# A 32-byte tile ahead of one buffer group: the weight buffers of the feed-forward stage start 32 bytes lower in SBUF

## The chip, the cores and the metric

One core of a Trainium2 chip runs the whole program. Times are device microseconds (us) of one execution; a profiled execution also gives a trace with start and duration of every instruction. SBUF is the on-chip working memory, 128 partitions wide. An address below is a byte offset within a partition, as the built program lays the tiles out. Engines: PE = TensorE (matmuls; its weight loads have a row of their own, PEld), DVE = VectorE, ACT = ScalarE, POOL = GpSimd, SP = SyncE, which issues most DMAs.

## The reference

One encoder layer on two sequences of 1024 tokens, width 1024: low-rank attention with 4 heads beside a Fourier mixing branch, one shared output projection, then a SwiGLU feed-forward block. All in float32.

```
x = x + ga1 * (concatenate([y_mla, y_four], axis=-1) @ w_out)
h2 = rmsnorm(x, g_ffn) * (1.0 + sc2) + sh2
ffn = (jax.nn.silu(h2 @ w_gate) * (h2 @ w_up)) @ w_down        # 1024 -> 2816 -> 1024
x = x + ga2 * ffn                                               # then a last rmsnorm
```

## The kernel before

**Products.** float32 values are split into a high part (rounded to the PE's fp32r type) and a low remainder: `split` (L63 on ACT, L64 on DVE). Each product of two split operands is a triple of matmuls, `mm3`: L79 high x high, L80 high x low, L81 low x high. In `mm3(out, lh, ll, rh, rl)` the l operands are the stationary weights, 128 x 128, loaded ahead of each matmul, and the r operands stream through as the moving operand, 128 x 512.

**Stages.** Up to about 300 us: modulation vectors, input projection, Fourier branch. About 300 to 750 us: attention (scores at L1216 to L1220, whose moving operand is `lat`, and whose weights are `qa` and `qp`) and the output projection (moving `wv`, weights `o0b`, `o1b`). Then the feed-forward block, for sequence 0 and then for sequence 1, with a Strassen-like scheme of 7 products in place of 8:

- The gate/up stage has 22 steps n, one for each 128 of the 2816 hidden columns. A step runs 7 products (`step`, `prod`) of 4 triples each. The moving operand is `H[k]`, kept in SBUF for the whole stage; the weights are `wh`, `wl`, made anew for each product by `hl`. So both sequences together have 2 x 22 x 7 x 4 = 1232 triples. POOL and DVE form the combinations of the weights (`rgu`, `val`) for the next step. During sequence 0 POOL also prepares combinations of `w_down` (`down_combos`, buffer `tdb`).
- The down stage has products of 11 chunks (`prod2`) with 4 triples each, where both operands are `wh` and `wl` tiles. The last product of sequence 1 uses operands that were split ahead and kept in the tiles of `H` (`held`).

**Where the tiles lie.** The pool of `w` (L1359, "p5", with the `H` tiles, `X0` and `X1`, the latter two holding `rgu` and later `draw`) sits at the lower end of SBUF from address 11840; each of its tiles has 8192 bytes in a partition, so all of them start at a multiple of 64. The pool of `w5` (L1501, "p5b") is allocated from the upper end, 229344, which is 32 above a multiple of 64. From the top down it holds 18 `val` buffers of 2048 bytes (lowest at 192480), 8 `wl` buffers of 2048, `ga`/`tdb` and `gf` of 4096 each, and 8 `wh` buffers of 2048. `wl` therefore begins at 176096 and `wh` at 151520; all of the pool lies 32 above a multiple of 64. The order in which the tags of `w5` are first asked for is set inside `hl`.

`hl` waits for nothing of its own: `wh` and `wl` have 8 buffers each, a step uses 7, and a product's pair is made while the same product of the step before runs. The instruction order is the program's own, held by `tc.issue_after` and `first` at some places.

Of the kernel before, what the change touches and what calls it, by code (L numbers as in the profile page):

```python
# [12 lines left out]
F32 = mybir.dt.float32  # L13
# [8 lines left out]
P = 128  # L22
# [31 lines left out]
def hybrid_encoder_kernel(ctx: ExitStack, tc: tile.TileContext, a: dict):  # L54
# [4 lines left out]
    def rd(t):  # L59
        return t.bitcast(F32)  # L60

    def split(hi, lo, src, eng=None):
        here["a"] = nc.scalar.copy(hi, src).ins  # L63
        here["v"] = (eng or nc.vector).tensor_tensor(out=lo, in0=src, in1=rd(hi), op=ALU.subtract).ins  # L64
# [751 lines left out]
    S = {}  # L816
# [541 lines left out]
    with ExitStack() as st:  # L1358
# [142 lines left out]
        w5 = st.enter_context(tc.tile_pool(name="p5b", bufs=1, side="right", reuse_waits="tile"))  # L1501
# [8 lines left out]
        def hl(v):  # L1510
            h = w5.tile([P, 512], F32R, tag="wh", name="wh", bufs=8)
            if "gf" not in S:
                S["gf"] = w5.tile([P, D], F32, name="gf")
                w5.tile([P, 2, 512], F32, tag="ga", name="tdb", bufs=1)
            l = w5.tile([P, 512], F32R, tag="wl", name="wl", bufs=8)
            split(h, l, v)
            return h, l

# [3 lines left out]
        for s in range(2):  # L1522
# [71 lines left out]
            if s == 0:  # L1594
                wts = [hl(w0[i]) for i in range(4)]
                with behind():
                    for _ in range(2):
                        next(prep)
            else:
                wts = first_w  # L1600
            A = {}
            late = None
            for n, f in enumerate(order):
# [10 lines left out]
                def step(j, ps, k, first, src=src):  # L1614
                    prod(ps, k, cur[j], first)
                    if s == 0 and n == 0:
                        if j == 0:
                            cur.extend(hl(v) for v in w0[4:])
                            w0.clear()
                            S["n3"] = norm3(1, S.pop("jk3").bitcast(BF16))  # L1620
# [11 lines left out]
                        for i in ((), (), (), (0, 1), (2, 3), (4,), (5, 6))[j]:  # L1632
                            nxt.append(hl(src[i]))
# [351 lines left out]
```

## Time and profile before

| | |
|---|---|
| Median of 3 runs | 2051.51 us (2048.66 to 2051.56) |
| Profiled execution, own time | 2051.31 us |
| Its span, first to last instruction | 2049.5 us |
| Mean granted PE clock | 0.996 |
| Gate/up, sequence 0 and 1 | about 750 to 1155 and 1390 to 1835 us |
| Down, sequence 0 and 1 | about 1155 to 1390 and 1835 to 2049 us |

In the rows of the trace, "L79 PE MATMUL bank<-H,wh" is an instruction of line 79 on PE that writes a tile named bank from H and wh; L81's rows name wl as the weight. A matmul's recorded duration runs past the start of the next one, since matmuls are pipelined; the distance from one start to the next tells what one costs. Three numbers with strokes are the shortest, the median and the longest duration in ns.

### The profile page before, as it was taken

What the parts mean: (1) busy time and instruction counts of PE and PEld (TensorE: products, weight loads), DVE (VectorE), ACT (ScalarE), POOL (GpSimd) and SP (SyncE); (2) the same over time, 40 slices, a digit from 0 to 9 for tenths busy, and PEclk for the clock granted to TensorE, in tenths of its full rate; (3) what the DMA queues carried; (4) which work ended last, traced back from release to release, by engine and by line L of the source; (5) the groups of instructions that cost most, each with busy time, mean ns of one, the idle gap of its engine ahead of it and who ended that gap; (6) DMA issues with size and microseconds to landing.
All of it is one profiled execution on the core that took longest, in us unless ns stands there. A gap on an engine that the chain in (4) does not pass through costs nothing.

```text
span 2049.5 us, 28369 instructions
## 1 busy us (share of the span) xinstructions
PE 2006.0 (98%) x9910; PEld 1641.6 (80%) x9910; DVE 1397.2 (68%) x2076; ACT 890.5 (43%) x1732; POOL 827.0 (40%) x972
## 2 busy tenths in 40 slices
PE   7899999999999999999999999999999999999998
PEld 3778778888888878888888888877888888888876
DVE  4568758666677778767777577688665665667585
ACT  2675436555555563333232365454323333336441
POOL 0564213112313237878878311234544444420142
PEclk9999999999999999999999999999999999999999
DMA  9786884444544475555455587674322322258662
GB/s 387 256 317 211 293 307 116 111 99 113 146 102 143 139 268 202 174 194 186 174 172 186 168 305 249 216 233 162 132 93 88 117 90 103 94 182 277 221 231 95
DMA packets 183036, 376.64 MB, mean 184 GB/s; under 512 B 17996, under 2 KB 57548, under 8 KB 179052
## 3 DMA queue, kind: packets, MB, share of 16 engines
q1 hardware_dynamic: 165548, 321.33, 45.9%
q0 software_dynamic: 17344, 53.49, 8.7%
q8 instruction: 78, 1.28, 0.2%
q14 instruction: 66, 0.54, 0.1%
HBM read 262.75 MB, written 120.39 MB: 187 GB/s over the span
## 4 chain that ended last, share of the span: by engine, by line
PE 55%; DVE 3%; DMA 2%; issue 1%; POOL 1%; ACT 0%; SPq 0%; DVEq 0%; ACTq 0%; POOLq 0%
PE bank L81 18%; PE bank L79 18%; PE bank L80 18%; DVE wl L64 1%; DVE val L137 1%; DMA draw<-s_d 1%; POOL val L137 0%; DMA val<-x_d 0%; DVE val L1782 0%; DMA draw<-t_d 0%; ACT wh L63 0%; DVE val L134 0%; POOL rs_y L105 0%; DVE H L64 0%; DMA rgu<-in_wgu_dram 0%
## 5 line engine op out<-in xcount | busy, mean ns | idle before, releaser
L79 PE MATMUL bank<-H,wh 128*128 128x512 f32 x1232 | 487.5, 396 | 2.4 <-DVE val L137 0.9
L81 PE MATMUL bank<-H,wl 128*128 128x512 f32 x1232 | 488.6, 397 | 0.2 <-DVE wl L64 0.2
L80 PE MATMUL bank<-H,wh 128*128 128x512 f32 x1232 | 484.4, 393 | 0.3 <-DVE H L64 0.3
L79 PEld LDWEIGHTS bank<-H,wh 128*128 128x128 f32 x1232 | 231.2, 188 | 58.6 <-DVE val L137 1.8
L80 PEld LDWEIGHTS bank<-H,wh 128*128 128x128 f32 x1232 | 231.3, 188 | 58.1 <-DVE H L64 0.6
L81 PEld LDWEIGHTS bank<-H,wl 128*128 128x128 f32 x1232 | 231.3, 188 | 56.9 <-DVE wl L64 0.5
L64 DVE TENSOR_TENSOR wl<-draw,wh 128x512 fp32r<-128x512 f32 x286 | 202.7, 743 | 85.6 <-ACT wh L63 85.2
L137 DVE TENSOR_TENSOR val<-bank,val 128x512 f32<-128x512 f32 x200 | 136.7, 689 | 158.8 <-PE bank L81 153.4
L63 ACT CAST wh<-draw 128x512 fp32r<-128x512 f32 x286 | 168.6, 619 | 159.3 <-PE bank L80 82.9
L137 POOL TENSOR_TENSOR val<-val 128x512 f32<-128x512 f32 x58 | 84.0, 1456 | 365.5 <-DVE val L1756 188.8
L80 PE MATMUL bank<-wl,wh 128*128 128x512 f32 x572 | 223.6, 391 | 2.3 <-DVE wl L64 2.3
L63 ACT CAST wh<-rgu 128x512 fp32r<-128x512 f32 x172 | 106.8, 621 | 269.5 <-PE bank L80 209.5
L81 PE MATMUL bank<-wh,wl 128*128 128x512 f32 x572 | 222.6, 389 | 0.0
L79 PE MATMUL bank<-wh 128*128 128x512 f32 x572 | 222.6, 389 | 0.0
L63 ACT CAST wh<-val 128x512 fp32r<-128x512 f32 x133 | 82.2, 621 | 269.8 <-PE bank L80 253.1
L64 DVE TENSOR_TENSOR wl<-val,wh 128x512 fp32r<-128x512 f32 x133 | 130.8, 985 | 77.3 <-ACT wh L63 77.3
L64 DVE TENSOR_TENSOR wl<-rgu,wh 128x512 fp32r<-128x512 f32 x172 | 166.8, 970 | 3.7 <-ACT wh L63 3.7
L134 POOL TENSOR_TENSOR val<-rgu 128x512 f32<-128x512 f32 x80 | 117.7, 1472 | 100.9 <-DMA rgu<-in_wgu_dram 97.2
L80 PEld LDWEIGHTS bank<-wl,wh 128*128 128x128 f32 x572 | 107.3, 188 | 27.4 <-DVE wl L64 5.4
L79 PEld LDWEIGHTS bank<-wh 128*128 128x128 f32 x572 | 107.4, 188 | 22.4
L81 PEld LDWEIGHTS bank<-wh,wl 128*128 128x128 f32 x572 | 107.4, 188 | 22.2
L1225 DVE TENSOR_REDUCE mx<-ps_s 128x1 f32<-128x1024 f32 x64 | 78.2, 1222 | 61.3 <-PE ps_s L1220 60.9
(385 smaller groups left out, 4048.4 us busy)
## 6 DMA issues: line engine op xcount, KB each, us to landing
rgu<-in_wgu_dram SPq DMA_DIRECT2D x86, 512.0 KB, 4.4
draw<-s_d SPq DMA_DIRECT2D x143, 256.0 KB, 3.8
s_d<-val POOLq DMA_DIRECT2D x88, 256.0 KB, 3.9
draw<-t_d SPq DMA_DIRECT2D x88, 256.0 KB, 4.2
s_d<-val SPq DMA_DIRECT2D x66, 256.0 KB, 2.4
draw<-in_w_down_dram SPq DMA_DIRECT2D x55, 256.0 KB, 4.6
wada<-in_w_ada_dram SPq DMA_DIRECT2D x11, 1024.0 KB, 10.5
xt<-in_x_dram SPq DMA_DIRECT2D x16, 512.0 KB, 10.3
```

The costliest lines, as they stand in the source:

```text
L63: here["a"] = nc.scalar.copy(hi, src).ins
L64: here["v"] = (eng or nc.vector).tensor_tensor(out=lo, in0=src, in1=rd(hi), op=ALU.subtract).ins
L79: nc.tensor.matmul(out, lh, rh, start=first, stop=False, skip_group_check=cont)
L80: nc.tensor.matmul(out, lh, rl, start=False, stop=False, skip_group_check=cont)
L81: here["t"] = nc.tensor.matmul(out, ll, rh, start=False, stop=last, skip_group_check=cont).ins
L134: return eng.tensor_tensor(out=out, in0=x, in1=y, op=ALU.subtract).ins
L137: eng.tensor_tensor(out=out, in0=x, in1=y, op=ALU.add)
L1225: nc.vector.tensor_reduce(out=mx, in_=ps, axis=AX.X, op=ALU.max)
```

## The change

```
             l = w5.tile([P, 512], F32R, tag="wl", name="wl", bufs=8)
+            if "edge" not in S:
+                S["edge"] = w5.tile([P, 8], F32, name="edge")
             split(h, l, v)
```

`edge` has 8 float32 values, 32 bytes, in a partition. It is asked for once, after the `wl` buffers, and lies between the lowest `val` buffer and the highest `wl` buffer, at 192448. Nothing reads or writes it. The `val` buffers and the tiles of `w` keep their places. `wl` now begins at 176064, `ga`/`tdb` at 171968, `gf` at 167872, `wh` at 151488: all four groups 32 bytes lower, and at multiples of 64.

No instruction is added, removed or moved on any engine. The pool before it in the same space (output projection: `wv0` from 155616 to 172000, `wv1` up to 188384) is now overlapped 32 bytes off its tile borders, so two first uses wait differently. On SP, at the head of the feed-forward stage, where the first `tdb` and `gf` are loaded, before:

```order
L1528 DMA val<-in_wgu_dram 128x512 [waits DMAHW5_49]
L1528 DMA val<-in_wgu_dram 128x512 [waits DMAHW6_49]
L1528 DMA val<-in_wgu_dram 128x512 [waits DMAHW7_49,PE_49]
L1551 DMA tdb<-in_w_down_dram 128x1024 [waits DMAHW0_49,PE_49]
L1690 DMA gf<-in_g_final_dram 128x1024 [waits DMAHW1_49,PE_49]
```

and after the change (its line numbers are 2 higher):

```order
L1530 DMA val<-in_wgu_dram 128x512 [waits DMAHW5_49]
L1530 DMA val<-in_wgu_dram 128x512 [waits DMAHW6_49]
L1530 DMA val<-in_wgu_dram 128x512 [waits DMAHW7_49,PE_49]
L1553 DMA tdb<-in_w_down_dram 128x1024 [waits DMAHW0_49,PE_49]
L1692 DMA gf<-in_g_final_dram 128x1024 [waits DMAHW1_49]
```

`tdb` now touches `wv0` as well as `wv1` and waits for one matmul more of the output projection (PE's count 4190 in place of 4189); POOL's first operation on `tdb` does too. `gf` needs no wait on PE any more, since `tdb`, ahead of it on SP, has already waited for that matmul.

## The prediction

> **What bounds the kernel now.** I read the page first: busy shares, then the chain that ended last.
>
> ```profile
> span 2049.5 us, 28369 instructions
> PE 2006.0 (98%) x9910; PEld 1641.6 (80%) x9910; DVE 1397.2 (68%) x2076; ACT 890.5 (43%) x1732; POOL 827.0 (40%) x972
> PE 55%; DVE 3%; DMA 2%; issue 1%; POOL 1%; ACT 0%; SPq 0%; DVEq 0%; ACTq 0%; POOLq 0%
> ```
>
> PE is busy for 98% of the span and leads the chain. So the question is what a matmul costs, not who waits. The busy time by stages (PE alone; start and end, busy us, count, granted clock, DMA share, GB/s) says it more sharply: two stretches of gate/up, one of down.
>
> ```profile
> 800.00:1100.00 300.00, 300.00 (x1288) 1.00 0.53 183
> 1440.00:1740.00 300.00, 300.00 (x1288) 1.00 0.29 103
> 1170.00:1290.00 120.00, 120.00 (x529) 1.00 0.77 264
> ```
>
> PE never stops in any of them and the clock is full, but gate/up starts 1288 matmuls in 300 us, some 233 ns each, and down 529 in 120 us, some 227 ns. All are 128 x 128 by 128 x 512. The rows by line give the exact period, from the first and the last start and the count: gate/up of sequence 0, of sequence 1, down, and the last product, where both operands are tiles of `H`.
>
> ```profile
> L79 PE MATMUL bank<-H,wh x429: 392/392/392, 799.9 to 1099.5; 128*128 128x512 f32 x143
> L79 PE MATMUL bank<-H,wh x429: 399/399/399, 1439.9 to 1739.5; 128*128 128x512 f32 x143
> L79 PE MATMUL bank<-wh x148: 389/389/389, 1189.7 to 1289.6; 128*128 128x512 f32 x148
> L79 PE MATMUL bank<-H x20: 389/389/389, 2026.7 to 2039.6; 128*128 128x512 f32 x20
> ```
>
> A triple (L79, L80, L81) takes 299.6/428 = 0.7000 us in gate/up, in both sequences, 99.9/147 = 0.6796 us in down and 12.9/19 = 0.679 us in the last product. Within a row every duration is the same, shortest to longest, although DMA, DVE and POOL load differ widely between the stretches. So the extra 20.4 ns are no contention with another engine that comes and goes; they belong to what PE itself reads.
>
> What differs is the address of the two operands. Take each address modulo 64. Down: weights and moving operand both at 32. Last product: both at 0. Gate/up: weights at 32 (`wh`, `wl`), moving operand at 0 (`H`). Writing into one bank many times is not the reason: the last product does that too. Neither 0 nor 32 is slow by itself; the case in which the two differ is.
>
> The attention scores test this inside one loop. Their weights `qa` and `qp` lie at 0 modulo 64 in both sequences; the moving `lat` lies at 0 for sequence 0 and, in other tiles, at 32 for sequence 1. First and last matmul of an undisturbed run of each:
>
> ```profile
> 302.51 0.39 PE L1219 MATMUL ps_s<-lat,qp 128*128 128x512 f32 x1
> 306.14 0.39 PE L1220 MATMUL ps_s<-lat,qp 128*128 128x512 f32 x1
> 539.70 0.39 PE L1216 MATMUL ps_s<-lat,qa 128*128 128x512 f32 x1
> 541.81 0.40 PE L1220 MATMUL ps_s<-lat,qp 128*128 128x512 f32 x1
> ```
>
> Sequence 0: 16 periods in 3.63 us, 0.2269 us each. Sequence 1: 9 periods in 2.11 us, 0.2344 us. The same lines with weights at the same place cost 7.5 ns more per matmul when the moving operand is 32 bytes off the weights' phase. Gate/up has 0.7000/3 = 0.2333, down 0.6796/3 = 0.2265: the same two levels. That is the ground of the forecast, with one reservation. Over the whole of both sequences the recorded durations of one such line (sequence 0, then 1) lie closer:
>
> ```profile
> L1219 PE MATMUL ps_s<-lat,qp x64: 387/393/397, 302.5 to 503.2; 128*128 128x512 f32 x64
> L1219 PE MATMUL ps_s<-lat,qp x62: 392/394/400, 513.1 to 714.8; 128*128 128x512 f32 x62
> ```
>
> The shortest differ by 5 ns, the medians by 1. There other shapes interrupt the scores every few periods; nothing interrupts gate/up, so the undisturbed runs weigh more.
>
> **The change part by part.**
>
> *Gate/up weights against H.* `wh` and `wl` move from 32 to 0 modulo 64, `H` stays at 0, and the phases agree as they do in down. At down's period a triple saves 0.7000 - 0.6796 = 0.0204 us; 1232 triples save 25.1 us. PE is 100% busy there, so nothing hides it: it comes off the end, unless another engine becomes late. The next in line, over each whole gate/up stage (PE, PEld, DVE, ACT, POOL busy):
>
> ```profile
> 750.00:1155.00 405.00, 403.58 (x1736) 324.20 (x1735) 300.30 (x304) 137.09 (x228) 310.96 (x280) 1.00 0.54 186
> 1390.00:1835.00 445.00, 443.96 (x1904) 356.82 (x1903) 280.97 (x344) 140.79 (x243) 205.11 (x191) 1.00 0.32 111
> ```
>
> Half of the saving, 12.6 us, falls on the first row: 405 becomes 392, of which POOL is busy 311 (79%) and DVE 300 (77%). Each pair of weights is made a whole step ahead, 28 x 0.7 = 19.6 us. I cost new waits at nothing; without this cover POOL would have to grow by 81 us before it set the pace.
>
> *A finer offset.* Take weights minus moving operand modulo 512 bytes, one row of a weight tile. It is 0 in down and in the last product, 416 in gate/up now, 384 after the change. No 512-column run at 384 is in the trace. The Fourier projection has short runs of 256 columns whose moving `wcs` steps by 2144 bytes, so that the offset changes from triple to triple. Here is the start of three such triples, each with the start that follows it:
>
> ```profile
> 133.84 0.28 PE L79 MATMUL bank<-wcs_h,eoh 128*128 128x256 f32 x1
> 134.22 0.28 PE L79 MATMUL bank<-wcs_h,eoh 128*128 128x256 f32 x1
> ...
> 134.93 0.28 PE L79 MATMUL bank<-wcs_h,eoh 128*128 128x256 f32 x1
> 135.28 0.28 PE L79 MATMUL bank<-wcs_h,eoh 128*128 128x256 f32 x1
> ...
> 136.32 0.28 PE L79 MATMUL bank<-wcs_h,eoh 128*128 128x256 f32 x1
> 136.68 0.36 PE L79 MATMUL bank<-wz_h,eoh 128*128 128x448 f32 x1
> ```
>
> The first triple has offsets 160, 416, 160 and takes 0.38 us; the second, 384, 128, 384, takes 0.35; the third, 0, 256, 0, takes 0.36. So 384 is as good as 0 here, and the slow one is that with 416. I take 384 as 0. The bounds are the rivals below: nothing gained, or 10 ns a triple better still.
>
> *Down weights and moving operand.* Both shift by 32, so the offset stays 0. Their common phase goes from 32 to 0, which the last product already has: 0.679 against 0.6796. Cost 0, with bounds of 0.6 ns on 572 triples, 0.3 us either way.
>
> *Splits.* DVE reads its first input at the old place and `wh` at the new one. Rows of the first down stage: `draw` at 0 with `wh` at 32, and `H` tiles at 0 alone.
>
> ```profile
> L64 DVE TENSOR_TENSOR wl<-draw,wh x153: 678/689/1811, 1165.4 to 1389.4; 128x512 fp32r<-128x512 f32 x153
> L64 DVE TENSOR_TENSOR H<-H,H x24: 679/686/1850, 1188.9 to 1231.1; 128x512 fp32r<-128x512 f32 x24
> ```
>
> Medians of 689 and 686 ns: at most 3 ns on some 600 splits, 1.8 us of DVE time that lies beside PE. Cost 0. The same answer holds for ACT's casts, POOL's work on `tdb` and the loads into `tdb`, `gf` and `ga`: same sizes, off PE's path, in stages where POOL and ACT have 94 and 268 of 405 us free.
>
> *Waits at the head.* The first `tdb` load and POOL's first `tdb` operation wait for one more matmul of the output projection. Its last low x high matmul on PE, the load's issue on SP, POOL's operation:
>
> ```profile
> 747.82 0.39 PE L81 MATMUL gb<-wv,o1b 128*128 128x512 f32 x1
> 750.86 0.99 SPq L1551 DMA_DIRECT2D tdb<-in_w_down_dram  x1
> L134 POOL TENSOR_TENSOR tdb<-tdb x1: 2282/2282/2282, 759.5 to 759.5; 128x512 f32<-128x512 f32 x1
> ```
>
> The matmul ends at 748.2, 2.6 us before SP comes to that load, and POOL comes 9 us later still. Queued behind the load on SP are `gf`, which nobody needs before the down stage, and `X0`. Cost 0; without the cover, one matmul, 0.23 us.
>
> Sum: -25.1 us. The profiled execution took 2051.31 us, 1.8 outside its span and 0.2 under the median of the runs, so 2051.3 - 25.1 = **2026.2 us**.
>
> **The rivals.**
>
> 1. *Part of it.* Agreeing phases need not give down's period. The input projection (448 columns) has weights and moving operand both at 0 modulo 64, with offsets 0 and 256. Four of its triples, and six 256-column matmuls to take the cost of a column from:
>
> ```profile
> 138.74 0.36 PE L79 MATMUL bank<-wz_h,eoh 128*128 128x448 f32 x1
> 141.17 0.36 PE L79 MATMUL bank<-wz_h,eoh 128*128 128x448 f32 x1
> 306.37 0.28 PE L79 MATMUL gb<-ql,wq_h 128*128 128x256 f32 x1
> 306.96 0.28 PE L81 MATMUL gb<-ql,wq_l 128*128 128x256 f32 x1
> ```
>
> A triple takes 2.43/4 = 0.6075 us. 256 columns take 0.59/5 = 0.118, so a column costs (0.2269 - 0.118)/256 = 0.43 ns, and 448 columns at the fast level would make a triple of 3 x (0.2269 - 64 x 0.00043) = 0.598. It has 9 ns more. If gate/up settles there, it saves 11 ns on each of 1232 triples, 14 us: **2037 us**. The medians of L1219, 1 ns apart, would put the low end of this at 3 ns a triple, 3.7 us, or 2047.6.
>
> 2. *Nothing.* The 20 ns stem from something that the shift leaves alone, such as the distance of the two pools in SBUF: **2051.3 us**. For it: in down and in the last product both operands lie in one pool, in gate/up in two. Against it: the three `wcs` triples above use the same tiles and take different times. [...]
>
> 3. *Slower.* The offset counts modulo 512 and 384 is worse than 416 at 512 columns. Place: every gate/up triple. Price: as much above today's as today's is above down's, 20.4 ns x 1232 = 25.1 us, **2076 us**. It decides from 3.3 ns a triple on (4.1 us). Against it: 0.35 us at 384 and 0.38 at 416 with 256 columns.
>
> 4. *More.* 384 beats 0, as 0.35 against 0.36 would have it; 5 to 10 ns a triple more, 6 to 12 us: **2014 to 2020 us**.
>
> **How the numbers follow.** Forecast 0.64 (its own range 2023 to 2030), part 0.14, nothing 0.10, more 0.08, slower 0.04. From 2018 to 2042 lie the forecast, most of "part" and some of "more": about 0.8. A measurement of this kernel tells 0.2%, 4.1 us, from no change. Faster by more: 0.64 + 0.08 + 0.13 of "part" = 0.85. Within: 0.10 and 0.01 of "part" = 0.11. Slower: 0.04.
>
> **What would show it.** The first and last start of L79 in a stretch of gate/up: 0.680 us a triple if I am right, 0.700 if nothing happens, 0.689 for part, 0.72 for slower; some 1323 matmuls in 300 us in place of 1288. Gate/up shorter by 12 to 13 us in each sequence; the down stages, and all before 745 us, as long as now. DVE's and ACT's medians in the splits within 5 ns. It would be wrong if the triple changes by another amount, if PE begins to wait for `wl` or `val` inside gate/up, or if the down triple leaves 0.680.

## The result, and the profile after

The changed kernel takes **2050.26 us** (median of 12 runs, 2046.51 to 2054.73) and the kernel before 2051.66 us (median of 12 runs, 2048.66 to 2055.99): ratio 0.9994, 95% interval 0.9984 to 1.0004. That is no change that can be measured. The forecast was 2026.2, with a range from 2018 to 2042, so it was wrong by the whole expected gain. The profiled execution took 2049.49 us itself.

From the page of the changed kernel, the span and the busy shares, and from the view by stretches of time the same three stretches as before (busy time of PE, PEld, DVE, ACT and POOL, then granted clock, DMA share, GB/s):

```profile
span 2047.7 us, 28368 instructions
PE 2002.2 (98%) x9910; PEld 1641.1 (80%) x9910; DVE 1386.5 (68%) x2076; ACT 891.3 (44%) x1732; POOL 831.1 (41%) x972
```

```profile
800.00:1100.00 300.00, 300.00 (x1288) 241.34 (x1287) 211.15 (x216) 90.89 (x152) 237.87 (x215) 1.00 0.53 183
1440.00:1740.00 300.00, 300.00 (x1292) 243.26 (x1292) 173.56 (x215) 91.30 (x154) 149.01 (x125) 1.00 0.29 102
1170.00:1290.00 120.00, 120.00 (x529) 99.09 (x528) 84.86 (x125) 65.95 (x117) 13.25 (x12) 1.00 0.76 259
```

PE is as full as before and the clock is full. Gate/up of sequence 0 starts 1288 matmuls in 300 us, exactly as before; 1323 were expected. Sequence 1 has 1292, four more. The rows of L79 in the changed kernel, for gate/up of sequence 0 and 1, for down, and for the last product (count, then shortest/median/longest duration in ns, then first and last start):

```profile
L79 PE MATMUL bank<-H,wh x429: 392/398/398, 800.2 to 1099.8; 128*128 128x512 f32 x143
L79 PE MATMUL bank<-H,wh x430: 390/393/404, 1440.3 to 1739.4; 128*128 128x512 f32 x144
L79 PE MATMUL bank<-wh x148: 389/389/389, 1189.9 to 1289.8; 128*128 128x512 f32 x148
L79 PE MATMUL bank<-H x27: 389/389/389, 2020.1 to 2037.8; 128*128 128x512 f32 x27
```

A triple takes 299.6/428 = 0.7000 us in sequence 0, 299.1/429 = 0.6972 in sequence 1, 99.9/147 = 0.6796 in down and 17.7/26 = 0.68 in the last product. The average of sequence 0 has not moved by a nanosecond, and yet the shift did reach PE: before, each L79 there had the one duration 392; now the durations alternate between 392 and 398. Something in the rhythm changed, and the mean did not. That the mean of sequence 1 fell by 2.8 ns is worth 616 x 0.0028 = 1.7 us, less than what runs of one kernel differ by.

### The profile page after: what moved, and what is told of

The parts are those of the page before. It is cut to its first block, busy times and chain, and to the rows that moved or that the text cites. A ratio compares the mean times of both kernels' runs of the same rounds, so it can differ in the third digit from the quotient of the medians.

```text
span 2047.7 us, 28368 instructions
## 1 busy us (share of the span) xinstructions
PE 2002.2 (98%) x9910; PEld 1641.1 (80%) x9910; DVE 1386.5 (68%) x2076; ACT 891.3 (44%) x1732; POOL 831.1 (41%) x972
## 4 chain that ended last, share of the span: by engine, by line
PE 55%; DVE 3%; DMA 2%; issue 1%; POOL 1%; ACT 1%; SPq 0%; DVEq 0%; ACTq 0%; POOLq 0%
PE bank L80 18%; PE bank L81 18%; PE bank L79 18%; DVE wl L64 1%; DVE val L137 1%; DMA draw<-s_d 1%; DMA val<-x_d 0%; POOL val L137 0%; DMA draw<-t_d 0%; DVE val L1784 0%; ACT wh L63 0%; DVE val L134 0%; DMA X<-hc_d 0%; POOL rs_y L105 0%; DVE val L1773 0%
## 5 line engine op out<-in xcount | busy, mean ns | idle before, releaser
L79 PE MATMUL bank<-H,wh 128*128 128x512 f32 x1232 | 486.8, 395 | 2.3 <-DVE val L137 1.0
L80 PE MATMUL bank<-H,wh 128*128 128x512 f32 x1232 | 486.5, 395 | 0.3 <-DVE H L64 0.3
L81 PE MATMUL bank<-H,wl 128*128 128x512 f32 x1232 | 486.3, 395 | 0.2 <-DVE wl L64 0.2
L79 PEld LDWEIGHTS bank<-H,wh 128*128 128x128 f32 x1232 | 231.7, 188 | 59.1 <-DVE val L137 1.9
L81 PEld LDWEIGHTS bank<-H,wl 128*128 128x128 f32 x1232 | 231.7, 188 | 55.7 <-DVE wl L64 0.5
L80 PEld LDWEIGHTS bank<-H,wh 128*128 128x128 f32 x1232 | 231.7, 188 | 55.5 <-DVE H L64 0.6
L137 POOL TENSOR_TENSOR val<-val 128x512 f32<-128x512 f32 x58 | 83.6, 1450 | 365.8 <-DVE val L1758 189.1
L80 PE MATMUL bank<-wl,wh 128*128 128x512 f32 x572 | 223.6, 391 | 4.1 <-DVE wl L64 4.1
L81 PE MATMUL bank<-wh,wl 128*128 128x512 f32 x572 | 222.7, 389 | 0.0
L79 PE MATMUL bank<-wh 128*128 128x512 f32 x572 | 222.6, 389 | 0.0
L64 DVE TENSOR_TENSOR wl<-rgu,wh 128x512 fp32r<-128x512 f32 x172 | 155.1, 902 | 3.7 <-ACT wh L63 3.7
L80 PEld LDWEIGHTS bank<-wl,wh 128*128 128x128 f32 x572 | 107.4, 188 | 29.6 <-DVE wl L64 7.3
L79 PEld LDWEIGHTS bank<-wh 128*128 128x128 f32 x572 | 107.4, 188 | 22.4
L81 PEld LDWEIGHTS bank<-wh,wl 128*128 128x128 f32 x572 | 107.4, 188 | 21.9
L134 POOL TENSOR_TENSOR val<-val 128x512 f32<-128x512 f32 x89 | 119.4, 1359 | 1.3
```

Source lines behind the costliest of these rows:

```text
L79: nc.tensor.matmul(out, lh, rh, start=first, stop=False, skip_group_check=cont)
L80: nc.tensor.matmul(out, lh, rl, start=False, stop=False, skip_group_check=cont)
L81: here["t"] = nc.tensor.matmul(out, ll, rh, start=False, stop=last, skip_group_check=cont).ins
L134: return eng.tensor_tensor(out=out, in0=x, in1=y, op=ALU.subtract).ins
L137: eng.tensor_tensor(out=out, in0=x, in1=y, op=ALU.add)
```

## Theories

The shift can have done nothing to the period for three reasons. **Distance:** the two addresses do not matter, the 20 ns come from the two pools as such, and the shift leaves the cause alone. **Modulus:** the offset between weights and moving operand matters, and only 0 is good, counted modulo 512 or 256; 384, which the change reached, is then still a disagreement. **Coarse places:** some offsets are good and some bad, in a way that is not just "0 or not". In what follows the offset is `wh` minus `H`, and "triple" is the period of L79 in a stretch of gate/up, as above. `wh_only` and `h_up` put the tile `edge` elsewhere, and `e160_p3` adds a second tile; all the other kernels change only the size of `edge`.

## The experiments

### e416 and e160: offset 0, and offset 256

`edge` of 416 bytes brings the offset to 0; 160 bytes bring it to 256, which is 0 modulo 256 only.

```
-                S["edge"] = w5.tile([P, 8], F32, name="edge")
+                S["edge"] = w5.tile([P, 104], F32, name="edge")
```

> The untouched tile has 416 bytes in place of 32, so that the weights' offset to the moving H, modulo 512, is 0 (before: 416; after the change: 384). Theory A, the offset modulo 512 decides: the gate/up triple falls to the down stage's 0.680 us and the time to about 2026 us. Theory B, the distance of the two pools or the structure of the gate/up loop decides: triple 0.700 us, about 2050 us, whatever the offset.

```
-                S["edge"] = w5.tile([P, 8], F32, name="edge")
+                S["edge"] = w5.tile([P, 40], F32, name="edge")
```

> Offset 256 modulo 512, a tile of 160 bytes. Theory A in its coarse form (only 0 is good): triple 0.697 to 0.700 us, about 2050 us. If multiples of 256 count as 0: 0.680 us and 2026 us. Theory B: 0.700 us.

e416: 2031.52 us (4 runs, 2029.97 to 2032.15) against 2053.32 of the kernel before on the same chip (7 runs), ratio 0.9895, interval 0.9878 to 0.9911. e160, a single run: 2030.68 us. L79 in gate/up of sequence 1, first e416, then e160:

```profile
L79 PE MATMUL bank<-H,wh x441: 389/389/389, 1440.3 to 1739.5; 128*128 128x512 f32 x147
```

```profile
L79 PE MATMUL bank<-H,wh x442: 389/389/389, 1440.1 to 1740.0; 128*128 128x512 f32 x148
```

299.2/440 = 0.6800 and 299.9/441 = 0.6800 us a triple: down's period, and down's one duration, 389. So the offset does set the period of gate/up, which is against "distance". And 256 is as good as 0 here, 0.6800 against 0.6800, so the modulus is not 512.

What becomes of the gain is read from the same run of e416. 1232 triples x 0.0200 are 24.6 us; the span fell by 2049.5 - 2028.1 = 21.4. The view of waits on PE from 745 us on (us in total, times, longest), three of its rows, of the kernel before and then of e416, where L1664 is the line that was L1662:

```profile
PE bank L80 <- DVE wl L64: 2.3, 3, 0.9
PE bank L79 <- DVE val L137: 0.9, 2, 0.5
...
PE bank L79 <- DVE val L1662: 0.5, 1, 0.5
```

```profile
PE bank L80 <- DVE wl L64: 2.1, 3, 0.9
PE bank L79 <- DVE val L1664: 1.9, 2, 1.7
PE bank L79 <- DVE val L137: 1.6, 2, 0.9
```

PE waits 1.9 + 1.6 - 0.5 - 0.9 = 2.1 us more for `val`, which DVE makes: a tenth of the gain goes into these waits. Of the remaining 1.1 us, 0.6 is a later start of gate/up (748.6 against 748.0 us); the rest is within what executions differ by.

### e288 and e64: two other offsets

```
-                S["edge"] = w5.tile([P, 8], F32, name="edge")
+                S["edge"] = w5.tile([P, 72], F32, name="edge")
```

> Offset 128 modulo 512, a tile of 288 bytes. If the sign of the offset makes no difference it should be as the changed kernel with 384 (0.697 to 0.700 us, about 2050 us). Theory A with multiples of 128 counting as 0 is already excluded by 384. Theory B: 0.700 us.

```
-                S["edge"] = w5.tile([P, 8], F32, name="edge")
+                S["edge"] = w5.tile([P, 16], F32, name="edge")
```

> Offset 352 modulo 512, phase 32 modulo 64 as before the change, a tile of 64 bytes. If the phase modulo 64 has any part in it, the fixed pattern of three as before, 0.700 us. If each offset has a period of its own, another value between 0.680 and 0.720 us. Theory B: 0.700 us.

e288 (offset 128): 2048.52 us, a single run. e64 (offset 352, or 96 modulo 256): 2056.24 us, a single run. Gate/up of sequence 0, e288 and then e64:

```profile
L79 PE MATMUL bank<-H,wh x430: 390/393/404, 800.3 to 1099.4; 128*128 128x512 f32 x144
```

```profile
L79 PE MATMUL bank<-H,wh x427: 392/397/400, 800.2 to 1099.6; 128*128 128x512 f32 x143
```

299.1/429 = 0.6972 and 299.4/426 = 0.7028 us. Offset 128 repeats what the changed kernel (384, the same modulo 256) has in sequence 1, down to the three durations 390/393/404. No phase modulo 64 is left as an explanation: 128 and 384 are both 0 modulo 64 and slow, 0.6972 us in e288 and 0.7000 and 0.6972 in the changed kernel.

### wh_only: two of the three operand pairs agree

The tile stands between `wh` and `gf`, so that only `wh` moves (offset 0), and `wl` keeps 160.

```
             if "gf" not in S:
+                S["edge"] = w5.tile([P, 40], F32, name="edge")
                 S["gf"] = w5.tile([P, D], F32, name="gf")
...
             l = w5.tile([P, 512], F32R, tag="wl", name="wl", bufs=8)
-            if "edge" not in S:
-                S["edge"] = w5.tile([P, 8], F32, name="edge")
             split(h, l, v)
```

> The tile has 160 bytes and lies between the wh buffers and gf, so that only wh moves: its offset to H modulo 256 becomes 0, that of wl stays 160, and wh and wl stand 160 apart. Theory N: a matmul pays when the weights loaded during it (those of the next matmul) are off the moving operand it reads. Then one of three gate/up matmuls pays (L80, before wl), the triple is about 0.687 us, and down keeps 0.680, since every load there still agrees. Theory O: a matmul pays when its own weights are off. Then L81 pays in gate/up (also 0.687), and in down L80 and L81 pay, 0.693. Time by N about 2036 us, by O about 2044 us.

A single run: 2058.89 us, beside 2050.43 of the kernel before. The three lines of gate/up of sequence 1, and then L79 of down:

```profile
L79 PE MATMUL bank<-H,wh x429: 396/397/398, 1440.2 to 1739.8; 128*128 128x512 f32 x143
```

```profile
L80 PE MATMUL bank<-H,wh x429: 393/396/396, 1439.7 to 1739.3; 128*128 128x512 f32 x143
```

```profile
L81 PE MATMUL bank<-H,wl x429: 392/392/396, 1440.0 to 1739.6; 128*128 128x512 f32 x143
```

```profile
L79 PE MATMUL bank<-wh x129: 389/393/397, 1190.3 to 1279.3; 128*128 128x512 f32 x129
```

Gate/up stays at 299.6/428 = 0.7000 us, although two of three matmuls read weights at offset 0. Down, whose `wh` and `wl` no longer agree with each other, goes to 89.0/128 = 0.695. In down two of the three pairs disagree: L80, whose weights are `wh` and whose moving operand is a `wl` tile, and L81, where it is the other way round. Both theories of the expectation fall: neither a price on each matmul with its own weights nor a price on each with the weights loaded for the next gives a full 0.7000 with two of three pairs in agreement. In gate/up one disagreeing pair in the triple costs the whole price of 20 ns; in down two of them cost 15. Beside the trace of the kernel before, whose span is 7.6 us shorter, down takes 3.0 us more in sequence 0 and 3.8 in sequence 1 from its first to its last L79. That is 6.8 us, where 15 ns on each of 572 triples would be 8.6, so not all of the price shows in the time. Gate/up also begins 1.2 us later.

### h_up: the other side moves

The weights stay where the kernel before has them, 32 above a multiple of 64; the tiles of `H` go up by 160 bytes to meet them.

```
+        S["edge"] = w.tile([P, 40], F32, name="edge")
         for tag in ("H20", "X0", "X1", "H21", "H30", "H31", "H00", "H41", "H01", "H50", "H51", "H10", "H11", "H40", "H60", "H61"):
...
-            if "edge" not in S:
-                S["edge"] = w5.tile([P, 8], F32, name="edge")
```

> The other operand is moved instead: a tile of 160 bytes stands at the head of the lower pool, so that H, X0 and X1 lie 160 bytes higher and wh and wl stay where they were before the change. Offset modulo 256 is 0, phase of the weights 32 modulo 64 and of H 32. If only the offset counts: gate/up triple 0.680 us, about 2031 us. If the weights' own address counts: 0.700 us and 2051 us.

A single run: 2036.22 us, beside 2050.43 of the kernel before. Gate/up of sequence 1:

```profile
L79 PE MATMUL bank<-H,wh x442: 389/389/389, 1439.8 to 1739.7; 128*128 128x512 f32 x148
```

299.9/441 = 0.6800 us, the period that e160 has with the weights moved by the same 160 bytes. So in gate/up it is the offset between the two and not the place of either. (The time stands above e416's because this execution came to gate/up later: its first matmul on `H` starts at 753.8 us, in e416 at 748.6. From there to the program's last matmul the two take 1271.2 and 1270.1 us.)

### e256, e192, e352, e384: what repeats, and whether any offset but 0 is good

```
-                S["edge"] = w5.tile([P, 8], F32, name="edge")
+                S["edge"] = w5.tile([P, 64], F32, name="edge")
```

> A tile of 256 bytes, offset 160 modulo 512. If the offset counts modulo 256, this is the kernel before to the last ns: triple 0.700 us with the same pattern of three, about 2051 us. If 512 is the modulus, it is a place of its own, between 0.680 and 0.705.

```
-                S["edge"] = w5.tile([P, 8], F32, name="edge")
+                S["edge"] = w5.tile([P, 48], F32, name="edge")
```

> A tile of 192 bytes, offset 224 modulo 256, 32 short of agreement. If the cost grows with the distance from agreement: between 0.680 and 0.697 us a triple, about 2040 us. If every disagreement costs the same: about 0.700 us, 2051 us.

```
-                S["edge"] = w5.tile([P, 8], F32, name="edge")
+                S["edge"] = w5.tile([P, 88], F32, name="edge")
```

> A tile of 352 bytes, offset 64 modulo 256. If only 0 is good: 0.697 to 0.703 us a triple, about 2050 us. If the curve is symmetric about 0 and grows with distance, below 0.700.

```
-                S["edge"] = w5.tile([P, 8], F32, name="edge")
+                S["edge"] = w5.tile([P, 96], F32, name="edge")
```

> A tile of 384 bytes, offset 32 modulo 256, the smallest disagreement on the other side of 0. Offset 224 gave 0.700 us. If only 0 is good: 0.697 to 0.703 us, about 2050 us.

Single runs: 2058.96 and 2053.32 us (beside 2050.43 of the kernel before), then 2058.65 and 2052.98 us (beside 2054.74). They differ by what lies ahead of the feed-forward stage: gate/up begins at 753.3, 748.7, 754.2 and 748.5 us, and from there to the program's last matmul all four take 1293 to 1294 us, the kernel before 1292. Gate/up of sequence 0 in e256, e192, e352, e384:

```profile
L79 PE MATMUL bank<-H,wh x429: 392/392/392, 799.7 to 1099.3; 128*128 128x512 f32 x143
```

```profile
L79 PE MATMUL bank<-H,wh x429: 393/394/397, 799.7 to 1099.3; 128*128 128x512 f32 x143
```

```profile
L79 PE MATMUL bank<-H,wh x429: 393/398/398, 799.7 to 1099.3; 128*128 128x512 f32 x143
```

```profile
L79 PE MATMUL bank<-H,wh x430: 395/396/396, 799.6 to 1099.9; 128*128 128x512 f32 x144
```

All four have 0.7000 us a triple. e256, a shift of exactly 256 from the kernel before, repeats even its one duration of 392. That confirms the modulus from a slow offset, as e160 did from the good one.

In sequence 1, e352 has the same mean in another form. Apart from one wait, every distance there is 233 or 234 ns, and the durations no longer alternate:

```profile
L79 PE MATMUL bank<-H,wh x428: 394/394/497, 1440.6 to 1739.6; 128*128 128x512 f32 x143
```

An even rhythm is thus no mark of the fast level, 0.680 us a triple; the distance from start to start tells.

The table gathers what the traces show. The last column is the pattern of the distances from one start to the next, in ns, read off consecutive starts of the trace, in sequence 0 where nothing else is said; a pattern repeats to 1 ns:

```
offset mod 256   kernels             triple, us   distances
0                e416, e160, h_up    0.680        226, 227, 227
32               e384                0.700        231 or 232, 235
64               e352 (seq. 0)       0.700        231, 235 or 236
64               e352 (seq. 1)       0.700        233 or 234
96               e64                 0.703        repeats after 7 matmuls
128              after (seq. 0)      0.700        229, 238
128              after (seq. 1)      0.697        repeats after 7 matmuls
128              e288                0.697        repeats after 7 matmuls
160              before, e256        0.700        231, 231, 238
224              e192                0.700        231, 235, 234, 234
0 and 160        wh_only             0.700        repeats after 9 matmuls
```

192 was not tried. The multiples of 32 that were tried fall into two classes: 0 with 0.680 us a triple, and the six others with 0.697 to 0.703.

### e160b and e160_p3: the gain timed, and the same cure tried in attention

e160b is e160 again. e160_p3 adds a 160-byte tile in the pool of the attention stage, so that `lat` of sequence 1 comes from offset 96 to 0 against `qa` and `qp`; the probabilities `pt`, the moving operand of the values, shift with it.

```
                 S["pt", s, b, h] = [w.tile([P, 8, 2, P], F32R, tag=f"pt{k}", name=f"pt{k}", bufs=2) for k in range(2)]
+            if "edge3" not in S:
+                S["edge3"] = w.tile([P, 40], F32, name="edge3")
...
-                S["edge"] = w5.tile([P, 8], F32, name="edge")
+                S["edge"] = w5.tile([P, 40], F32, name="edge")
```

> The kernel with a tile of 160 bytes once more, now timed in five rounds. From its profile, 616 triples in each sequence save 20 ns: 2026 to 2032 us where the kernel before takes 2051, ratio 0.988 to 0.991.

> The same, and an untouched tile of 160 bytes at the upper end of the attention pool as well, so that lat of sequence 1 and the probabilities pt lie 160 bytes lower: offset modulo 256 becomes 0 for the scores of sequence 1 (before 96) and for the values (before 96). If the rule holds outside the feed-forward stage, undisturbed scores of sequence 1 go from 0.2344 to 0.2267 us a matmul, and the time falls by 1 to 3 us more, to 2028 to 2030 us. If the rule is special to gate/up: scores stay at 0.234, time as e160b.

e160b: 2031.63 us (4 runs, 2030.19 to 2034.54) against 2054.74 of the kernel before (7 runs), ratio 0.9892, interval 0.9877 to 0.9907. e160_p3: 2030.11 us (4 runs, 2028.70 to 2031.03), ratio 0.9883, interval 0.9866 to 0.9899. Both are faster than both kernels of this case; the two cannot be told apart. The scores of sequence 1 and the values (weights `ckv`, moving `pt`) of both sequences, in e160b and then in e160_p3:

```profile
L1219 PE MATMUL ps_s<-lat,qp x64: 392/397/400, 509.9 to 719.2; 128*128 128x512 f32 x64
```

```profile
L79 PE MATMUL gb<-pt,ckv x256: 274/280/368, 323.1 to 735.2; 128*128 128x256 f32 x128
```

```profile
L1219 PE MATMUL ps_s<-lat,qp x62: 387/393/398, 512.0 to 714.0; 128*128 128x512 f32 x62
```

```profile
L79 PE MATMUL gb<-pt,ckv x256: 276/283/365, 317.9 to 730.1; 128*128 128x256 f32 x128
```

The scores, 512 columns wide, take the durations of sequence 0 (387/393/397 before). The values, 256 columns wide, whose `pt` moved along, get 3 ns longer in the median. The mean distances between neighbouring starts (those under 300 ns, and under 200 for the values) say the same: the scores of sequence 1 go from 233.8 to 230.8 ns, the level that sequence 0 has in both kernels (230.8 and 230.7), and the values go from 118.2 to 119.6. From the first to the last matmul of the values attention takes 735.2 - 323.1 = 412.1 us in the one kernel and 730.1 - 317.9 = 412.2 in the other, and the expected 1 to 3 us are not seen there. The two changes are of one size: 320 score matmuls gain 3.0 ns each, some 1 us, and 768 value matmuls lose 1.3 to 1.4 ns each, some 1 us.

The expected 0.2267 us is not reached either. Here is the run of ten scores in e160_p3 that stands in the place of the prediction's run in sequence 1, first and last matmul:

```profile
539.04 0.40 PE L1216 MATMUL ps_s<-lat,qa 128*128 128x512 f32 x1
541.12 0.39 PE L1220 MATMUL ps_s<-lat,qp 128*128 128x512 f32 x1
```

Its 9 periods take 2.08 us, 0.2311 us each, at offset 0. The kernel before took 0.2344 there, at offset 96.

## Why the prediction was wrong, point by point

- **What bounds the kernel** held. PE is full, and the operands' addresses set the period: 0.7000 and 0.6800 us in kernels that differ by nothing but where tiles lie.
- **The step that failed is "A finer offset", in the words "I take 384 as 0".** 384 is as slow as 416, at 0.7000 and 0.6972. What the runs showed in its place: 0.680 us a triple at 0 modulo 256, and 0.697 to 0.703 at each of the six other offsets tried. The choice rested on three triples with 256 columns, read at 10 ns each, and the 256-column matmuls that the runs tried went the other way than those with 512: in e160_p3 the values went from 118.2 to 119.6 ns each, where the scores of sequence 1, 512 columns wide, went from 233.8 to 230.8. The prediction had said itself that the trace holds no 512-column run at 384. What it did have could not decide: down, the last product and the scores of sequence 0 all lie at offset 0, which agrees by every modulus, so each of them fits "modulo 64" and "modulo 256" alike; and the slow rows, 416 and the 96 of the scores of sequence 1, disagree by every modulus. "The phases agree as they do in down" was a step from offset 0 to 384 that no row carried.
- **The scores as a test** were weaker than they looked. The two runs of the prediction differ in more than the offset: at offset 0 the run of sequence 1 takes 0.2311 us (e160_p3), so of the 7.5 ns only 3.3 come from the offset, and 4.2 stand between two runs that both have offset 0. The averages over the two sequences of the kernel before, 230.8 and 233.6 ns, differ by 3 as well.
- **The price** was right: 20.4 ns a triple forecast, 20.0 measured in e416, e160 and h_up. Only the shift that earns it is another, 160 or 416 bytes in place of 32.
- **The cover** was nearly right. When the gain does come, PE waits 2.1 us more for `val`; the prediction had put new waits at nothing. The stage is longer than the row from 750 to 1155 us that the cover was read from: the first of its 616 triples starts at 748.0 and the last at 1183.5, and over this whole stretch POOL and DVE are busy 317 us each of 435.5, so the room was larger than stated. The stretch from 1170 to 1290 thus begins with 13 us of gate/up; the period of down was read from 1189.7 on and is not touched by it.
- **Down** held, 0.6796 us before and after. **Splits** held too. DVE's rows of the first down stage in the changed kernel:

```profile
L64 DVE TENSOR_TENSOR wl<-draw,wh x153: 676/689/1784, 1166.2 to 1388.9; 128x512 fp32r<-128x512 f32 x153
L64 DVE TENSOR_TENSOR H<-H,H x24: 676/685/1834, 1187.1 to 1229.0; 128x512 fp32r<-128x512 f32 x24
```

  The medians are 689 and 685 ns, where they were 689 and 686.
- **Waits at the head** held: the first matmul on `H` starts at 746.3 us, before the change at 748.0. In the other kernels it lies between 747.3 and 754.2, so this shows only that no long wait arose.
- **Rivals.** "Nothing" came true in its time, but not by its reason. It said that the shift leaves the cause alone, such as the distance of the pools; in h_up and e160 the pools lie as far apart as ever, and a shift of 160 bytes takes the whole 20 ns away. "Slower" fell in its ground as well: 256 is as good as 0 (0.6800 us a triple in e160 and in e416), so the period of gate/up does not count modulo 512. "Part" and "more" did not occur.

**What stays open** is the mechanism. The recorded weight loads do not get longer (in gate/up of sequence 0, 241.34/1287 = 0.1875 us each in the changed kernel and 247.88/1322 = 0.1875 in e416), so the time is not seen in the load itself. Why 256, why one disagreeing pair in a gate/up triple costs as much as three (0.7000 us in wh_only and before), and why the values with their 256 columns behave otherwise, no run here settles.

## What to carry to other kernels

Where the period of long runs of equal matmuls differs between stages at a full clock, compare the addresses of weights and moving operand, and try a tile of padding in steps until the stage has the period of the best one. In gate/up here, with 512 columns, a triple took 0.680 us where both weight tiles agreed with the moving operand modulo 256 bytes, 0.697 to 0.703 at the six other offsets, and 0.700 where `wh` alone agreed. The values, 256 columns wide, lost by the same agreement what the scores gained (118.2 to 119.6 ns each), so look at all the matmuls that a padding tile shifts. Before a forecast leans on agreement "modulo n", look for a row in which the candidates for n differ; if all agreeing examples have offset 0, they say nothing about n, and the range has to reach to no change with real weight.

## What the runs showed of the hardware

- In gate/up, with its long runs of 128 x 128 by 128 x 512 matmuls and a new weight load for each, the mean distance from start to start went with the weight address minus the moving operand's address, taken modulo 256 bytes: 226.7 ns at 0 (e416, e160, h_up), 232.4 to 234.3 ns at 32, 64, 96, 128, 160 and 224 (e384, e352, e64, the changed kernel and e288, the kernel before and e256, e192). In e160b, 0 in place of 160 takes 1.1% off the kernel's time (0.9892, interval 0.9877 to 0.9907).
- The longer period is no random loss. Where gate/up is slow, the distances repeat in cycles of 2, 3, 4, 7 or 9 matmuls, to 1 ns for 300 us (231, 231, 238 ns in the kernel before; 229, 238 in sequence 0 of the changed kernel), or are even (233 or 234 ns, e352 in sequence 1). The same offset can hold two cycles: 0.7000 in sequence 0 and 0.6972 in sequence 1 of the changed kernel.
